# Early start of a second output projection, and other engines for the last products, in a two-layer trunk kernel

## The chip, the cores and the metric

The kernel runs on one core of one Trainium2 chip. Its time is the device time of one execution in microseconds (us), and the number given for it is the median of several runs. A core has a matrix engine (TensorE, PE in the profile; its weight loads are PEld), three engines for the work between the products (VectorE or DVE, ScalarE or ACT, GpSimd or POOL) and SyncE (SP), which here only issues transfers (DMAs). Each engine works through its own queue of instructions in order; semaphores make one engine wait for another. Matmuls write PSUM, eight banks of 128 partitions by 512 floats; the rest of the data lies in SBUF.

## What is computed

A decoder trunk of two residual layers over 1024 tokens with 1024 features, and a final RMS norm. Layer 0 mixes with eight retention heads and eight RWKV-7 heads in parallel; their outputs are concatenated and go through one output projection. Layer 1 uses sliding-window attention. After each mixer comes a SwiGLU FFN.

```python
h = x
for layer in range(DEPTH):
    n = rms_norm(h, norm1_g[layer])
    if layer % 2 == 0:
        mix = retention_rwkv_mixer(n, ...)   # concat([ret_out, rwkv_out]) @ w_out
    else:
        mix = swa_sink_mixer(n, ...)
    h = h + mix
    n = rms_norm(h, norm2_g[layer])
    h = h + swiglu(n, ffn_w_gate[layer], ffn_w_up[layer], ffn_w_down[layer])
return rms_norm(h, final_g)
```

The RWKV group is a recurrence over time, `state = state * w + (state a) b + v k`, with one state of 64 by 64 for each head. The kernel works it out in chunks of 64 tokens. The two parts that the change touches are `concat([ret_out, rwkv_out]) @ w_out` added to `h`, and the final `rms_norm`.

## The kernel before

**Layout.** Everything is held transposed: features on the 128 partitions, tokens along the free axis. The tokens are split into two halves of 512 (`hf` 0 and 1, `HT = 512`), the features into eight blocks of 128 (`KT = 8`). So one block of one half is a tile of 128 by 512 floats, which fills one PSUM bank.

**Products.** Every large product is done in three matmuls on a fast format: an operand is split into a high part (a rounding cast on ScalarE) and a low part (the difference, on GpSimd or VectorE), and `hi*hi + hi*lo + lo*hi` is summed in PSUM. `split` (L339, L341) does this to data and `wsplit` (L318, L319) to weights, 512 columns of a weight at a time into one tile with the tag `w` (four buffers); the raw weights come into `wr` (two buffers of 1024 columns). `gemm` (L333 to L335) does a whole contraction of eight blocks, 24 matmuls; `prod` (L1118 to L1120) does a part of one, told whether it is the first or last part.

**Who orders the work.** The program is written once, in one order, and a planner with a timing model lays out each engine's queue ahead of time. An instruction that comes earlier in the program goes first if its inputs are there, and a later one may fill in. Buffers of a tag (`nq` has four, `f` in PSUM three) are handed out in the order of the program. Pools of tiles open and close like a stack on the left or the right of SBUF; a tile in a new pool waits for the readers of the old tiles that lay in its place.

**Layer 0's mixer** (`mixer0`, L379 to L441). All 16 heads of both halves run under a small schedule of their own (`Plan`). The RWKV heads come in four units `u` of two pairs: (half 0, pairs 0 and 1), (half 0, pairs 2 and 3), then the same for half 1. A unit's recurrence takes eight steps, one after the other; then come a group norm, a gate product and the multiplications at L926 to L928, which leave the output `y` of one pair (two heads) in a tile tagged `rt`. L929 stores it to `cats[hf][4 + p]` in HBM. The retention outputs go to `cats[hf][p]` (L1057). So the eight contraction blocks of half 1's projection are: four of retention, two of unit 2, and two (blocks 6 and 7) of unit 3, the last in time.

**The output projection** (`wout`, L547 to L564) loads the eight head outputs of a half into `nq` tiles, splits them into eight `n8` tiles, loads the residual input (`load8`, L368, on ScalarE's queue) and then does eight output blocks `d`: load and split the weights, `gemm` into a bank of the tag `f`, add to `h` on VectorE (L563).

**What stands around it.** In `trunk` half 0's projection is the last thing in `mixer0`. Then pool `nb` opens, the RMS factor of half 0 is formed (`factor_of`, `rstd`: squares on ScalarE at L349, sums on VectorE at L354, one product with a matrix of ones at L356, then Ln and Exp at L357 and L358; its squares and sums use the same four `nq` buffers), `form0` writes half 0's normalised blocks (L1067), stores them to `bd` (L1078) and splits them, and only then comes `wout(1, ...)`. Behind it are half 1's factor, the first FFN products (`early`, L1266 and L1269) and `form1`, half 1's forms for the FFN (a Strassen-like scheme with seven block products where the plain way has eight).

**The end.** `final_r` (L1541) squares the eight blocks of a half (L1549), scales them by the final gain (L1550), sums seven of the squares on VectorE (L1554), and multiplies the sum (L1557) and the eighth square (L1558) by the ones matrix, then Ln and Exp (L1560, L1561). `final_out` (L1564) multiplies each block by the factor (L1568), on the engine that a letter names (v for VectorE, p for GpSimd), and stores it (L1569). Half 0's factor is formed while the last products of half 1 (`down`) still run; their additions to `h` are at L1305.

```python
K.final_out(0, r0, order[0], "vpvpvpvp")
K.final_out(1, r1, order[1], "vpvvpvvv")
```

Of the kernel before, what the change touches and what calls it, by code (L numbers as in the profile page):

```python
# [13 lines left out]
ALU = mybir.AluOpType  # L14
# [186 lines left out]
class Kern:  # L201
# [172 lines left out]
    @staticmethod  # L374
    def kt(x):
        return lambda k: x[k // 4][:, k % 4, :]


    def mixer0(self):  # L379
# [23 lines left out]
        self.pr, self.st, self.rst, self.dns, self.nds = {}, {}, {}, {}, {}  # L403
# [34 lines left out]
        self.h[0] = self.wout(0, self.n8(self.pp), self.s8(self.hx, "h0", 2))  # L438
        gz.__exit__(None, None, None)
        gm.__exit__(None, None, None)  # L440
        return pq  # L441
# [105 lines left out]
    def wout(self, hf, n8, h8):  # L547

        nc = self.nc
        ch = []  # L550
        for k in range(KT):
            c = self.t(self.pp, [P, HT], "nq", 4)
            nc.sync.dma_start(c, self.cats[hf][k])
            a, b = self.hl(n8, k)
            self.split(c, a, b, k % 2 == 0)
            ch.append((a, b))
        h = self.load8(self.x_half(hf), h8)
        for d in range(KT):
            w = self.wload(self.A["w_out"][d])
            ps = self.pst("f", [P, HT])  # L560
            self.gemm(ps, w, ch)
            hk_ = self.kt(h)(d)
            nc.vector.tensor_tensor(out=hk_, in0=hk_, in1=ps, op=ALU.add)  # L563
        return h  # L564
# [201 lines left out]
    def unit(self, u, hf, pairs):  # L766
# [156 lines left out]
        for p, st, (y, q) in zip(pairs, sts, ys):  # L923
# [5 lines left out]
            nc.sync.dma_start(self.cats[hf][4 + p], y)  # L929
# [611 lines left out]
    def final_r(self, hf, pool, order):  # L1541
# [5 lines left out]
        for i, k in enumerate(order):  # L1547
# [3 lines left out]
            if i == 0:  # L1551
                acc = sq
            elif i < KT - 1:
                nc.vector.tensor_tensor(out=sq, in0=acc, in1=sq, op=ALU.add)  # L1554
                acc = sq
            if i == KT - 2:
                nc.tensor.matmul(ps, self.cst["ones"], acc, start=True, stop=False)  # L1557
        nc.tensor.matmul(ps, self.cst["ones"], sq, start=False, stop=True)  # L1558
# [13 lines left out]
def trunk(tc, A, out):  # L1572
    with ExitStack() as ctx:
        K = Kern(ctx, tc, A, out)

        pq = K.mixer0()
        gb, nb = K.pool("nb", "left")
# [42 lines left out]
        K.form0("n2a", K.factor_of(0, sp, "f"), K.n8(K.pp), sp)  # L1620
        K.h[1] = K.wout(1, K.n8(nb), K.s8(hy, "h1", 2))
# [52 lines left out]
        r0 = K.final_r(0, fz, order[0])  # L1674
        run(f)
        r1 = K.final_r(1, fz, order[1])
        K.final_out(0, r0, order[0], "vpvpvpvp")
        K.final_out(1, r1, order[1], "vpvvpvvv")
# [56 lines left out]
```

## Time and profile before

| | |
|---|---|
| median of 3 runs | 2510.35 us (2509.92 to 2510.72) |
| the profiled execution's own time | 2509.89 us |
| its span in the profile | 2507.3 us |
| granted TensorE clock, mean | 0.974 of full speed |
| VectorE, ScalarE, GpSimd busy | 65%, 41%, 53% of the span |
| the chain that ended last, by engine | PE 65%, DVE 14%, DMA 7%, ACT 5%, issue 4%, POOL 3% |
| DMA | 400.64 MB, mean 160 GB/s |

How to read it. The profile shows one execution. In an order of time, a row gives the start in us from the beginning of the span, the time from the first to the end of the last of the instructions merged in the row, the engine, the line of the kernel, what is written from what, the shape and the count; in square brackets stand the idle time of the engine just before it and what ended it. In the chain that ended last, each row is a piece of time that the end had to wait for: start, length, engine, tile and line. In a table by stretches the columns are the stretch, its length, the busy time and count of each engine, the granted clock, the busy share of the DMA engines and GB/s. Matmuls overlap: one takes 0.39 us from its start to its end, but they follow each other closer than that, so a row's length is not TensorE's pace. `w<-wr` means that a tile tagged `w` was written from one tagged `wr`.

### The profile page before, as it was taken

What the parts mean: (1) busy time and instruction counts of PE and PEld (TensorE: products, weight loads), DVE (VectorE), ACT (ScalarE), POOL (GpSimd) and SP (SyncE); (2) the same over time, 40 slices, a digit from 0 to 9 for tenths busy, and PEclk for the clock granted to TensorE, in tenths of its full rate; (3) what the DMA queues carried; (4) which work ended last, traced back from release to release, by engine and by line L of the source; (5) the groups of instructions that cost most, each with busy time, mean ns of one, the idle gap of its engine ahead of it and who ended that gap; (6) DMA issues with size and microseconds to landing.
All of it is one profiled execution on the core that took longest, in us unless ns stands there. A gap on an engine that the chain in (4) does not pass through costs nothing.

```text
span 2507.3 us, 35752 instructions
## 1 busy us (share of the span) xinstructions
PE 2368.3 (94%) x13106; PEld 1850.0 (74%) x13106; DVE 1631.8 (65%) x2395; ACT 1036.8 (41%) x1907; POOL 1320.2 (53%) x1048
## 2 busy tenths in 40 slices
PE   8899899899978999999999999899998999998996
PEld 6677677677756778887778776677786788886885
DVE  4765854765466248887675358557627788777776
ACT  5354433324354323333333545446634233333335
POOL 6556331312456547776576432252247577767664
PEclk9999999899989999999999999899999999999998
DMA  8565553343353545663464322142335456646652
GB/s 278 186 207 177 178 162 122 117 122 116 116 183 136 192 144 181 219 213 139 174 257 161 97 74 67 42 133 68 109 126 173 146 198 217 219 176 229 243 206 86
DMA packets 169037, 400.64 MB, mean 160 GB/s; under 512 B 43040, under 2 KB 45728, under 8 KB 168864
## 3 DMA queue, kind: packets, MB, share of 16 engines
q1 hardware_dynamic: 165744, 392.87, 45.9%
q10 hardware_dynamic: 2832, 4.45, 0.5%
q8 instruction: 104, 1.70, 0.3%
q0 software_dynamic: 288, 1.05, 0.1%
q14 instruction: 69, 0.57, 0.1%
HBM read 272.34 MB, written 120.59 MB: 157 GB/s over the span
## 4 chain that ended last, share of the span: by engine, by line
PE 65%; DVE 14%; DMA 7%; ACT 5%; issue 4%; POOL 3%; SPq 1%; DVEq 0%; ACTq 0%; POOLq 0%
PE ps_m L1118 5%; PE ps_m L1119 5%; PE ps_m L1120 5%; PE ps_f L232 5%; PE ps_f L334 5%; PE ps_f L333 5%; PE ps_f L335 5%; PE ps_m L232 4%; PE ps_f L1119 3%; PE ps_f L1118 3%; PE ps_f L1120 3%; PE ps_r L1118 2%; PE ps_r L1119 2%; PE ps_r L1120 2%; PE ps_c L1120 2%
## 5 line engine op out<-in xcount | busy, mean ns | idle before, releaser
L319 POOL TENSOR_TENSOR w<-wr,w 128x512 fp32r<-128x512 f32 (+1 forms) x276 | 370.4, 1348 | 475.8 <-ACT w L318 467.2
L232 PE MATMUL ps_f<-n,w 128*128 128x512 f32 x1440 | 388.0, 417 | 5.9 <-ACT n L447 3.7
L232 PEld LDWEIGHTS ps_f<-n,w 128*128 128x128 f32 x1440 | 269.7, 193 | 91.6 <-issue 25.5
L318 ACT CAST w<-wr 128x512 fp32r<-128x512 f32 (+1 forms) x276 | 167.2, 612 | 254.7 <-PE ps_f L335 141.9
L333 PE MATMUL ps_f<-n,w 128*128 128x512 f32 x496 | 200.0, 407 | 10.7 <-ACT n L339 7.7
L334 PE MATMUL ps_f<-n,w 128*128 128x512 f32 x496 | 200.0, 403 | 2.2 <-POOL n L341 1.6
L1118 PE MATMUL ps_f<-n,w 128*128 128x512 f32 x453 | 183.0, 406 | 16.1 <-ACT u L1267 10.6
L335 PE MATMUL ps_f<-n,w 128*128 128x512 f32 x496 | 196.7, 398 | 0.3 <-POOL w L319 0.3
L1119 PE MATMUL ps_f<-n,w 128*128 128x512 f32 x453 | 180.9, 399 | 8.5 <-DVE n L341 5.8
L1120 PE MATMUL ps_f<-n,w 128*128 128x512 f32 x453 | 180.7, 400 | 5.9 <-POOL w L319 5.9
L319 POOL TENSOR_TENSOR w<-wq,w 128x512 fp32r<-128x512 f32 x86 | 124.1, 1453 | 37.5 <-ACT w L318 20.8
L1125 DVE TENSOR_TENSOR nq<-ps_m,u 128x512 f32<-128x512 f32 x88 | 58.7, 684 | 113.3 <-PE ps_m L1120 113.3
L333 PEld LDWEIGHTS ps_f<-n,w 128*128 128x128 f32 x496 | 95.3, 193 | 36.2 <-ACT n L339 9.2
L341 POOL TENSOR_TENSOR n<-nq,n 128x512 fp32r<-128x512 f32 x69 | 115.7, 1688 | 11.0 <-ACT n L339 10.9
L1118 PEld LDWEIGHTS ps_f<-n,w 128*128 128x128 f32 x453 | 86.6, 191 | 46.0 <-ACT u L1267 16.1
L334 PEld LDWEIGHTS ps_f<-n,w 128*128 128x128 f32 x496 | 94.5, 191 | 28.8 <-issue 5.1
L335 PEld LDWEIGHTS ps_f<-n,w 128*128 128x128 f32 x496 | 94.5, 191 | 22.4 <-issue 1.9
L1119 PEld LDWEIGHTS ps_f<-n,w 128*128 128x128 f32 x453 | 86.8, 192 | 29.0 <-DVE n L341 6.5
L1120 PEld LDWEIGHTS ps_f<-n,w 128*128 128x128 f32 x453 | 87.0, 192 | 27.2 <-POOL w L319 7.6
L1118 PE MATMUL ps_m<-cb,w 128*128 128x512 f32 x232 | 93.7, 404 | 9.5 <-DVE nq L1125 9.5
L1279 POOL TENSOR_TENSOR w<-wd,w 128x512 fp32r<-128x512 f32 (+1 forms) x53 | 75.5, 1429 | 49.8 <-ACT w L1278 48.8
L1119 PE MATMUL ps_m<-cb,w 128*128 128x512 f32 x232 | 93.2, 402 | 0.0
(505 smaller groups left out, 6184.4 us busy)
## 6 DMA issues: line engine op xcount, KB each, us to landing
hc<-n SPq DMA_DIRECT2D x74, 512.0 KB, 2.6
wsp<-w SPq DMA_DIRECT2D x60, 512.0 KB, 3.3
w<-wsp SPq DMA_DIRECT2D x60, 512.0 KB, 3.8
wq<-in_w_gate SPq DMA_DIRECT2D x44, 512.0 KB, 4.4
u<-u SPq DMA_DIRECT2D x88, 256.0 KB, 2.9
n<-hc SPq DMA_DIRECT2D x43, 512.0 KB, 5.8
hid<-n SPq DMA_DIRECT2D x66, 256.0 KB, 2.1
ha<-hc SPq DMA_DIRECT2D x33, 512.0 KB, 6.0
```

The lines of the kernel that those rows point to most:

```text
L232: self.nc.tensor.matmul(out, lhsT, rhs, **kw)
L318: nc.scalar.copy(hi[:, :n], raw[:, c])
L319: nc.gpsimd.tensor_tensor(out=lo[:, :n], in0=raw[:, c], in1=hi.bitcast(F32)[:, :n], op=ALU.subtract)
L333: nc.tensor.matmul(ps, hi, rh, start=k == 0, stop=False)
L334: nc.tensor.matmul(ps, hi, rl, start=False, stop=False)
L335: nc.tensor.matmul(ps, lo, rh, start=False, stop=k == n - 1)
L341: e.tensor_tensor(out=lo, in0=src, in1=hi.bitcast(F32), op=ALU.subtract)
L1118: mm(ps, hi, xh, start=first and k == 0, stop=False, skip_group_check=True)
L1119: mm(ps, hi, xl, start=False, stop=False, skip_group_check=True)
L1120: mm(ps, lo, xh, start=False, stop=last and k == len(w) - 1, skip_group_check=True)
L1125: add = lambda o, x, y: V.tensor_tensor(out=o, in0=x, in1=y, op=ALU.add)
L1279: nc.gpsimd.tensor_tensor(out=lo, in0=v, in1=hi.bitcast(F32), op=ALU.subtract)
```

## The change

It has three parts.

1. **Head outputs.** The loading and splitting of the heads leaves `wout` and becomes `heads(hf, n8, have)`. For half 1 it is called at the end of `mixer0`, right after half 0's projection and before the pool of the mixer closes, so in the program it now stands before half 0's RMS factor. The two outputs of unit 3 are not stored to HBM and loaded again: their `rt` tiles are kept in `self.last` and split in place.
2. **Half 1's projection.** `wout(1, ch, ..., 2)` begins with three output blocks over the first six contraction blocks: `d = 0` and `1` over blocks 0 to 3, both over 4 and 5, then `d = 2` over 0 to 5; then all three over blocks 6 and 7; then the additions. The weights of `d = 0` and `1` are loaded and split in halves of 512 columns, so that both first halves come first. The other five blocks are done as before. The ones product of half 0's factor takes the PSUM tag `m` (four banks) in place of `f`, whose three banks the three open outputs hold.
3. **The end.** For half 1 only four squares are summed on VectorE; the other four go to the ones matrix one by one. All of half 0's last products go to GpSimd, and of half 1's one more.

```diff
@@ mixer0
-        self.h[0] = self.wout(0, self.n8(self.pp), self.s8(self.hx, "h0", 2))
+        self.h[0] = self.wout(0, self.heads(0, self.n8(self.pp)), self.s8(self.hx, "h0", 2))
         gz.__exit__(None, None, None)
+        gb, nb = self.pool("nb", "left")
+        ch = self.heads(1, self.n8(nb), self.last)
         gm.__exit__(None, None, None)
-        return pq
+        return pq, gb, nb, ch
@@ heads, wout
-    def wout(self, hf, n8, h8):
-
-        nc = self.nc
+    def heads(self, hf, n8, have=None):
+
         ch = []
         for k in range(KT):
-            c = self.t(self.pp, [P, HT], "nq", 4)
-            nc.sync.dma_start(c, self.cats[hf][k])
+            c = (have or {}).get(k)
+            if c is None:
+                c = self.t(self.pp, [P, HT], "nq", 4)
+                self.nc.sync.dma_start(c, self.cats[hf][k])
             a, b = self.hl(n8, k)
             self.split(c, a, b, k % 2 == 0)
             ch.append((a, b))
+        return ch
+
+    def wout(self, hf, ch, h8, late=0):
+
+
+        nc = self.nc
         h = self.load8(self.x_half(hf), h8)
-        for d in range(KT):
+        kt = self.kt(h)
+
+        def add(d, ps):
+            nc.vector.tensor_tensor(out=kt(d), in0=kt(d), in1=ps, op=ALU.add)
+
+        n = 3 if late else 0
+        if late:
+            parts = []
+            for o in (0, HT):
+                raw = self.t(self.pp, [P, 1024], "wr", 2)
+                for d in range(2):
+                    nc.sync.dma_start(raw[:, d * HT : d * HT + HT], self.A["w_out"][d][:, o : o + HT])
+                parts.append([self.wsplit(raw[:, d * HT : d * HT + HT], HT) for d in range(2)])
+            w = [parts[0][d] + parts[1][d] for d in range(2)] + [self.wload(self.A["w_out"][2])]
+            ps = [self.pst("f", [P, HT]) for _ in range(3)]
+            k = KT - late
+            for d, ks in ((0, (0, 4)), (1, (0, 4)), (0, (4, k)), (1, (4, k)), (2, (0, k)), *((d, (k, KT)) for d in range(3))):
+                c = slice(*ks)
+                self.prod(ps[d], w[d][c], ch[c], ks[0] == 0, ks[1] == KT)
+            for d in range(3):
+                add(d, ps[d])
+        for d in range(n, KT):
             w = self.wload(self.A["w_out"][d])
             ps = self.pst("f", [P, HT])
             self.gemm(ps, w, ch)
-            hk_ = self.kt(h)(d)
-            nc.vector.tensor_tensor(out=hk_, in0=hk_, in1=ps, op=ALU.add)
+            add(d, ps)
         return h
@@ unit
-            nc.sync.dma_start(self.cats[hf][4 + p], y)
+            if u < 3:
+                nc.sync.dma_start(self.cats[hf][4 + p], y)
+            else:
+                self.last[4 + p] = y
@@ final_r(self, hf, pool, order, n)
-            if i == 0:
-                acc = sq
-            elif i < KT - 1:
+            if 0 < i < n:
                 nc.vector.tensor_tensor(out=sq, in0=acc, in1=sq, op=ALU.add)
-                acc = sq
-            if i == KT - 2:
-                nc.tensor.matmul(ps, self.cst["ones"], acc, start=True, stop=False)
-        nc.tensor.matmul(ps, self.cst["ones"], sq, start=False, stop=True)
+            acc = sq
+            if i >= n - 1:
+                nc.tensor.matmul(ps, self.cst["ones"], sq, start=i == n - 1, stop=i == KT - 1)
@@ trunk
-        pq = K.mixer0()
-        gb, nb = K.pool("nb", "left")
+        pq, gb, nb, ch = K.mixer0()
...
-        K.form0("n2a", K.factor_of(0, sp, "f"), K.n8(K.pp), sp)
-        K.h[1] = K.wout(1, K.n8(nb), K.s8(hy, "h1", 2))
+        K.form0("n2a", K.factor_of(0, sp, "m"), K.n8(K.pp), sp)
+        K.h[1] = K.wout(1, ch, K.s8(hy, "h1", 2), 2)
...
-        r0 = K.final_r(0, fz, order[0])
+        r0 = K.final_r(0, fz, order[0], 7)
         run(f)
-        r1 = K.final_r(1, fz, order[1])
-        K.final_out(0, r0, order[0], "vpvpvpvp")
-        K.final_out(1, r1, order[1], "vpvvpvvv")
+        r1 = K.final_r(1, fz, order[1], 4)
+        K.final_out(0, r0, order[0], "pppppppp")
+        K.final_out(1, r1, order[1], "vpvvpvvp")
```

More of the change, by code (lines that the diff above doesn't have):

```diff
@@ L402, in mixer0 @@
         pq = self.psum("ps0", {"f": 3, "m": 4, "c": 1})
-        self.pr, self.st, self.rst, self.dns, self.nds = {}, {}, {}, {}, {}
+        self.pr, self.st, self.rst, self.dns, self.nds, self.last = {}, {}, {}, {}, {}, {}
         units = [(0, 0), (0, 2), (1, 0), (1, 2)]
@@ L1539, in w_o, with final_r @@
             )
-    def final_r(self, hf, pool, order):
+    def final_r(self, hf, pool, order, n):
         nc = self.nc
```

## The prediction

> **What bounds the kernel now.** I read the page first, then the chain that ended last between 590 and 860 us and from 2400 us on, then each engine's order of time at those two places.
>
> ```profile
> span 2507.3 us, 35752 instructions
> PE 2368.3 (94%) x13106; PEld 1850.0 (74%) x13106; DVE 1631.8 (65%) x2395; ACT 1036.8 (41%) x1907; POOL 1320.2 (53%) x1048
> ```
>
> TensorE (PE) is busy for 94%, so at most 139 us can be had by closing its gaps. The change touches two: the start of the second output projection and the end of the kernel. The first, in TensorE's order of time:
>
> ```profile
> 705.67 0.39 PE L335 MATMUL ps_f<-n,w 128*128 128x512 f32 x1
> 710.47 2.07 PE L356 MATMUL ps_f<-nq,c_ones 128*128 128x512 f32 x2 [4.41 <-DVE nq L354]
> 720.22 1.22 PE L333 MATMUL ps_f<-n,w 128*128 128x512 f32 x2 [7.67 <-ACT n L339]
> ```
>
> ```profile
> 769.42 0.39 PE L1118 MATMUL ps_f<-n,w 128*128 128x512 f32 x1
> ```
>
> The first projection issues its last matmul at 705.67 and ends at 705.9. The second begins at 720.2, when ScalarE (ACT) has cast its first head output, and gives way to the FFN at 769.4. Why so late, in SyncE's queue (SPq), ScalarE's order and the chain:
>
> ```profile
> 661.38 0.33 SPq L1057 DMA_DIRECT2D cat<-r  x1
> 667.59 32.90 SPq L293 DMA_DIRECT2D wr<-in_w_out  x6
> 703.58 5.21 SPq L929 DMA_DIRECT2D cat<-rt  x2
> 708.91 0.86 SPq L1205 DMA_DIRECT2D wq<-in_w_gate  x2
> 709.82 1.69 SPq L553 DMA_DIRECT2D nq<-cat  x3
> ```
>
> ```profile
> 668.76 1.15 ACT L349 ACTIVATE nq<-h 128x512 f32<-128x512 f32 x2
> ...
> 719.55 2.37 ACT L339 CAST n<-nq 128x512 fp32r<-128x512 f32 x4
> ```
>
> ```profile
> 707.75 0.69 DVE rt L928
> 708.43 0.61 DVE h L563
> 709.06 0.64 ACT nq L349
> 709.73 0.70 DVE nq L354
> ```
>
> The last retention output was stored at 661.4, yet even it is read back only after 709.8: the loads share the four `nq` buffers with the RMS sum of half 0, which comes first in the program and ends at 710.4 (L354). The last RWKV output is ready at 708.4 (L928). So two of eight contraction blocks are late, and six wait for buffers. The same time by stretches (length, then busy PE, PEld, DVE, ACT, POOL, granted clock, DMA share, GB/s):
>
> ```profile
> 660.00:706.00 46.00, 46.00 (x288) 34.83 (x283) 18.70 (x34) 21.15 (x31) 16.96 (x14) 1.00 0.37 126
> 710.00:720.00 10.00, 2.07 (x2) 0.50 (x2) 5.17 (x6) 6.42 (x9) 3.28 (x2) 0.50 1.04 396
> 720.00:726.00 6.00, 5.36 (x12) 3.77 (x13) 6.00 (x7) 2.44 (x6) 3.38 (x3) 0.50 0.86 287
> ```
>
> After the gap TensorE works 6 us at half clock, so the gap costs more than its length.
>
> **The change at the projection.** An output block takes 24 matmuls; two successive additions show its length when nothing is in the way:
>
> ```profile
> 758.74 0.69 DVE L563 TENSOR_TENSOR h<-h,ps_f 128x512 f32<-128x512 f32 x1 [2.83 <-PE ps_f L335]
> 764.18 0.69 DVE L563 TENSOR_TENSOR h<-h,ps_f 128x512 f32<-128x512 f32 x1 [2.83 <-PE ps_f L335]
> ```
>
> That is 5.44 us, 0.2267 a matmul, 43.5 for all 192. The new order does 54 of them first (three outputs over six blocks, 12.2 us), then 18 over the last two (4.1), then five outputs as before (27.2). If TensorE never waits, it runs on from 705.9: plus 43.5, plus the RMS matmul pair (2.07 at half clock above, so 1.0 at full) gives 750.4 instead of 769.4, a gain of 19.0.
>
> What must hold:
>
> *The six early heads.* Loads, casts and subtractions move ahead of the RMS sum. With a store and a load of about this landing time,
>
> ```profile
> hid<-n SPq DMA_DIRECT2D x66, 256.0 KB, 2.1
> ```
>
> the last one is back by 666, and the squares of half 0 begin at 668.8 now: the sum is hardly held up, and it has until 706 to catch up. The work is 6 casts of 0.6 on ScalarE, 3 subtractions on GpSimd (POOL) and 3 on VectorE (DVE) of at most 1.7 (rows below). It lies beside the first projection, 660 to 706, where TensorE is busy 46.00 of 46.00 and the three engines under half. Without that cover it costs at most 5 us. In SyncE's queue the loads pass the six projection weight loads and two of the FFN's; 1.5 MB at a DMA share of 0.37 is hidden. Two stores and two loads go.
>
> *The two late heads.* Split in place behind L928: a cast of 0.6 and a subtraction of at most 1.7 put the last at 710.7, and the late block is not reached before 718. That covers 7 us.
>
> *Weights.* Two of four weight loads become pairs of 256 KB, and two split tiles stay held until the late block. One half of the fourth output's weights waits for such a tile, released near 720; its cast and subtraction may stand behind one of half 0's forms:
>
> ```profile
> L319 POOL TENSOR_TENSOR w<-wr,w 128x512 fp32r<-128x512 f32 x18 | 25.1, 1404 | 22.4 <-ACT w L318 22.4
> L341 POOL TENSOR_TENSOR n<-u,n 128x512 fp32r<-128x512 f32 x4 | 6.9, 1730 | 10.5 <-ACT n L339 10.5
> ```
>
> 720 + 0.6 + 1.7 + 1.4 is 723.7, for a tile wanted at 722.6 or 725.3. Bounds 0 to 5 us; I take 3 with all small waits, as these rows miss by one at least.
>
> *Half 1's input* must have landed for the first addition, near 720:
>
> ```profile
> L368 ACTq DMA_DIRECT2D h<-in_xT x2: 374/374/374, 706.2 to 709.1; - x2
> ```
>
> ```profile
> DMA to landing us min/median/max: 5.0/7.2/9.3
> ```
>
> 718.4 at the latest now; 2 MB of head loads no longer crowd it, and its space is read 2 us longer. Nothing added. The RMS pair's new PSUM tag has buffers free since L928, before the pair can run: nothing.
>
> Gain: 19.0 - 3 = **16.0 us**. The work behind starts from the second projection's last addition, so I carry the gain to the end undiminished.
>
> On a wait that stays, the Trainium skill ("TensorE: Matmul & The Clock Gate", What's actually happening) says that about 3.4 us of sustained work restore the full clock. The rows here show some 6. A new idle stretch would so cost 1.7 us extra by the page (an estimate) and 3.0 by the rows; the rows decide.
>
> **The change at the end.** VectorE (two stretches), TensorE, ScalarE (two) and GpSimd (two) now:
>
> ```profile
> 2479.87 5.76 DVE L1568 TENSOR_TENSOR h<-h,y 128x512 f32<-128x512 f32 x4 [3.41 <-ACT y L1561]
> ```
>
> ```profile
> 2491.54 0.68 DVE L1305 TENSOR_TENSOR h<-h,ps_y 128x512 f32<-128x512 f32 x1
> 2497.81 5.84 DVE L1568 TENSOR_TENSOR h<-h,y 128x512 f32<-128x512 f32 x6 [5.59 <-ACT y L1561]
> ```
>
> ```profile
> 2483.44 0.39 PE L1120 MATMUL ps_y<-n,w 128*128 128x512 f32 x1
> ```
>
> ```profile
> 2492.25 0.63 ACT L1549 ACTIVATE nq<-h 128x512 f32<-128x512 f32 x1 [0.60 <-DVE h L1305]
> ```
>
> ```profile
> 2497.15 0.63 ACT L1561 ACTIVATE y<-y 128x512 f32<-128x512 f32 x1
> ```
>
> ```profile
> 2449.05 1.29 POOL L341 TENSOR_TENSOR n<-hr,n 128x512 fp32r<-128x512 f32 x1
> ```
>
> ```profile
> 2479.92 6.83 POOL L1568 TENSOR_TENSOR h<-h,y 128x512 f32<-128x512 f32 x4 [6.59 <-ACT y L1561]
> ```
>
> TensorE is done at 2483.8, but the last addition to half 1 runs at 2491.5, since four products of half 0 stand before it on VectorE. They go to GpSimd: the addition can run from 2483.8 to 2484.5. ScalarE has earlier squares and scalings to finish (0.5 late), then needs the same 5.5 us from the last square's start to the factor's end (2492.25 to 2497.78): 2485.0 + 5.5 is 2490.5 instead of 2497.8. The last four squares go to TensorE one by one, pairs of at most 2.1 us, as they arrive; the last pair lies in those 5.5 us as now.
>
> Then the last products, five on VectorE, three on GpSimd. GpSimd has eight of half 0 first, from 2479.9: 10.3 us at 1.29 alone, 13.7 at 1.71 (6.83/4) beside VectorE's. VectorE does additions from PSUM meanwhile, not those products, so I take 10.3: free at 2490.2. Three more at 1.71 end at 2495.6; VectorE's five at 1.44 (5.76/4) beside them and 0.7 after take some 6 us, to 2496.5. Now the last ends at 2503.65. Gain **7.2 us**; by the other bound 2498.9 and 4.8.
>
> The Trainium skill ("GPSIMD Engine Reference", Engine selection) speaks against this edit: for elementwise work it advises VectorE, GpSimd being about 2 times slower with two inputs. The rows agree, 1.29 against 0.68. By the page's factor eleven products of 1.36 (an estimate) would end at 2494.9, still before VectorE.
>
> **Sum.** 16.0 + 7.2 = 23.2 off the profiled execution's own 2509.89 (its span and 2.6 around it). That lies 0.46 under the median of 2510.35, hence **2487.2**.
>
> **The rivals.**
>
> *The banks.* Three outputs hold all three `f` PSUM banks; the fourth needs the first one's addition, on a VectorE queue that also carries half 0's forms, held up by a store. In the chain and in VectorE's order:
>
> ```profile
> 719.02 4.90 DMA bd<-u
> ```
>
> ```profile
> 728.26 3.47 DVE L341 TENSOR_TENSOR n<-u,n 128x512 fp32r<-128x512 f32 x2
> ```
>
> Behind them, at 731.7, output four starts at 732.4, not 723: 9.3 lost and 3.0 of half clock, 2499.5. For: VectorE is busy 6.00 of 6.00 from 720 to 726. Against: four of the head subtractions leave that stretch.
>
> *The change doesn't do what it says:* if the new tiles become free only with the last head's, at 708.4, six casts and three subtractions hold TensorE until about 712, some 6 and 1 of half clock: 2494.2. Against: their space is what the retention part and the inner pool leave, done by 661.4.
>
> *The FFN swallows it.* Half 1's forms keep VectorE full after the projection:
>
> ```profile
> 800.00:810.00 10.00, 6.48 (x15) 4.57 (x15) 10.00 (x9) 4.31 (x8) 8.72 (x6) 0.58 0.31 109
> ```
>
> TensorE waits here and falls to 0.58. If this stretch ended when it does now, only 7.2 would stay: 2503.2, give or take 3. Against: it starts from half 1's factor, which waits for the projection.
>
> *GpSimd ends last*, at 2498.9: 2489.6.
>
> *Slower.* TensorE takes its queue in order, so the first of the 18 late matmuls blocks all behind it. If the last head's split stood behind half 0's forms, the price is 1 us for each beyond 718 and 3 of half clock. It eats the 23 when the split lands at 738 and ends slower by over 0.2% beyond 743: 2516 or more. For: it needs the same two queues; the forms' end at 731.7, a second wait of 4.9 for a store and its own 2.3 are 739. Against: it is ready at 708.4, before any form.
>
> **How the numbers follow.** Forecast 0.53, GpSimd last 0.07, banks 0.16, not done as said 0.07, FFN 0.12, slower 0.05. A measurement here tells some 0.2%, 5 us, from no change: the bound for faster is 2505.3. FFN lies half on each side of it: faster 0.89, same 0.06, slower 0.05. The forecast's own bounds, 0 to 5 for the small waits and 1 at the tail, give 2484 to 2490. The range goes to 2482, since waits behind the projection may fall by 2, and up to 2500 to hold the banks; the FFN and the slower case, 0.17, are left out.
>
> **What would show it.** No TensorE gap over 2 us between 706 and 751, clock 1.00; first L1118 at 751 to 755; the six head loads before 670; the last addition within 1 us of TensorE's last product, the last multiplication about 13 us after it instead of 20. Wrong would be: TensorE waiting in the late block for the split, a fourth output waiting for a bank, or the shift at L1118 not found again at the end.

## The result and the profile after

The changed kernel takes 2485.91 us (median of 4 runs, 2481.93 to 2489.24) beside 2510.53 (4 runs, 2509.92 to 2511.55): a ratio of 0.9901, 95% interval 0.9884 to 0.9918, or 24.6 us less. The forecast was 2487.2 us.

The page of the profiled execution (2481.93 us):

```profile
span 2480.2 us, 35757 instructions
PE 2357.5 (95%) x13112; PEld 1844.5 (74%) x13112; DVE 1623.6 (65%) x2387; ACT 1036.0 (42%) x1907; POOL 1324.5 (53%) x1053
```

TensorE is busy for 10.8 us less than before (2368.3) and idle for 16.3 us less; the span is 27.1 us shorter. The line numbers have moved: L341, L349 and L356 are as before, the additions of the projection are now L570 (L563 before), half 0's forms L1099 (L1067), the products of `prod` L1150 to L1152 (L1118 to L1120), the last multiplications L1598 (L1568).

TensorE at the join of the two projections, in order of time: the last four products of the RWKV heads' gates, the first product of the second projection, half 0's RMS pair, the one gap, the FFN's first product:

```profile
695.05 1.88 PE L232 MATMUL ps_m<-gl,gup 128*128 128x512 f32 x4
...
700.41 0.39 PE L1150 MATMUL ps_f<-n,w 128*128 128x512 f32 x1
...
707.62 1.13 PE L356 MATMUL ps_m<-nq,c_ones 128*128 128x512 f32 x2
...
721.43 0.47 PE L333 MATMUL ps_f<-n,w 128*128 128x512 f32 x1 [3.39 <-ACT n L339]
...
748.76 0.39 PE L1150 MATMUL ps_f<-n,w 128*128 128x512 f32 x1
```

The second projection starts in the matmul after the first one's last, not 14 us later, and passes half 0's RMS pair, which runs at 707.62 behind its first 31 products. The gap of 3.39 us comes at the fourth output, behind the late block. The row names a cast as what ended it, but VectorE shows what the output had to wait for, a free `f` bank:

```profile
711.84 3.78 DVE L1099 SCALAR_TENSOR_TENSOR u<-h,pv,rs 128x512 f32<-128x512 f32 x4 [4.28 <-ACT rs L358]
715.55 3.47 DVE L341 TENSOR_TENSOR n<-u,n 128x512 fp32r<-128x512 f32 x2
718.94 1.74 DVE L1099 SCALAR_TENSOR_TENSOR u<-h,pv,rs 128x512 f32<-128x512 f32 x1
720.61 0.67 DVE L570 TENSOR_TENSOR h<-h,ps_f 128x512 f32<-128x512 f32 x1
```

The first addition to half 1, which empties the first of the three banks, stands behind seven of half 0's forms and subtractions. It ends at 721.28; TensorE goes on at 721.43.

What feeds the early start, in the changed kernel: SyncE's last three loads of early heads, and then, on ScalarE, the last early head's cast and the last late one's:

```profile
658.22 3.88 SPq L556 DMA_DIRECT2D nq<-cat  x3
```

```profile
668.75 0.60 ACT L339 CAST n<-nq 128x512 fp32r<-128x512 f32 x1
...
704.23 0.62 ACT L339 CAST n<-rt 128x512 fp32r<-128x512 f32 x1 [2.28 <-DVE rt L957]
```

The last of the six early heads is cast at 668.75, 31 us before it is wanted; the last head in place at 704.23, against its use in the late block near 714 (54 products of 0.2267 and the RMS pair after 700.41).

The end of the kernel: TensorE's last product, VectorE, ScalarE's last square, GpSimd.

```profile
2461.98 0.39 PE L1152 MATMUL ps_y<-n,w 128*128 128x512 f32 x1
```

```profile
2462.40 0.69 DVE L1337 TENSOR_TENSOR h<-h,ps_y 128x512 f32<-128x512 f32 x1 [0.32 <-PE ps_y L1152]
2470.11 6.30 DVE L1598 TENSOR_TENSOR h<-h,y 128x512 f32<-128x512 f32 x5 [7.02 <-ACT y L1591]
```

```profile
2463.49 0.61 ACT L1582 ACTIVATE nq<-h 128x512 f32<-128x512 f32 x1
2464.14 0.72 ACT L1583 ACTIVATE h<-h,pv 128x512 f32<-128x512 f32 x1
2464.76 0.61 ACT L1582 ACTIVATE nq<-h 128x512 f32<-128x512 f32 x1
2465.41 0.72 ACT L1583 ACTIVATE h<-h,pv 128x512 f32<-128x512 f32 x1
2466.15 1.28 ACT L1590 ACT_TABLE_LOAD   x1
```

```profile
2458.45 10.38 POOL L1598 TENSOR_TENSOR h<-h,y 128x512 f32<-128x512 f32 x8 [6.59 <-ACT y L1591]
2470.15 5.11 POOL L1598 TENSOR_TENSOR h<-h,y 128x512 f32<-128x512 f32 x3 [1.32 <-ACT y L1591]
```

The last addition follows the last product at once, and the last multiplication ends 14.0 us after that addition began (2476.41 less 2462.40). ScalarE now works without a pause; its last square starts 1.7 us after the addition has ended.

**Where the time went.** For every kernel I read the same marks from its trace. *Lead-in*: from the span's start to the first product of the first output projection, which no kernel here changes. *Projection*: from the start of the last gate product (0.59 us before the end of the row at 695.05) to ScalarE's first copy of an FFN product (`u<-ps_f`, at 751.68 in the trace after); it holds the join, the second projection and the FFN's first product, 55.34 us here. *Tail*: from the start of TensorE's last product to the span's end. In us, with the medians of all runs and the ratio to the kernel before on the same chip:

| kernel | lead-in | projection | tail | span | median (runs) | ratio, 95% interval |
|---|---|---|---|---|---|---|
| before | 627.8 | 70.97 | 23.89 | 2507.3 | 2510.53 (4) | |
| after | 624.0 | 55.34 | 18.18 | 2480.2 | 2485.91 (4) | 0.9901, 0.9884-0.9918 |
| after again | 630.9 | 56.86 | 18.19 | 2493.6 | 2487.24 (4) | 0.9920, 0.9895-0.9944 |
| tail only | 627.2 | 71.01 | 18.49 | 2497.6 | 2501.71 (7) | 0.9971, 0.9958-0.9984 |
| projection only | 625.8 | 55.30 | 24.84 | 2491.3 | 2497.67 (6) | 0.9962, 0.9946-0.9978 |
| in place, plain order | 622.4 | 58.42 | 18.63 | 2488.5 | 2490.43 (4) | 0.9933, 0.9918-0.9948 |
| through HBM, late block | 623.0 | 58.21 | 19.14 | 2486.9 | 2489.89 (4) | 0.9928, 0.9900-0.9955 |
| through HBM, plain order | 621.0 | 55.00 | 18.55 | 2477.1 | 2484.47 (4) | 0.9919, 0.9888-0.9950 |
| two in place, six late | 626.8 | 72.99 | 18.73 | 2501.6 | 2503.39 (10) | 0.9969, 0.9950-0.9987 |
| sum in other buffers | 624.1 | 70.00 | 18.47 | 2491.9 | 2504.63 (10) | 0.9976, 0.9960-0.9992 |
| sum in an `f` bank | 626.3 | 61.82 | 18.18 | 2490.8 | 2494.61 (4) | 0.9952, 0.9933-0.9970 |
| two open outputs | 622.8 | 53.42 | 18.47 | 2478.8 | 2487.52 (4) | 0.9919, 0.9889-0.9949 |
| ... and scaling on VectorE | 625.1 | 53.44 | 21.14 | 2490.6 | 2490.99 (5) | 0.9924, 0.9896-0.9951 |
| ... and scaling behind squares | 625.8 | 53.41 | 21.07 | 2491.6 | 2489.29 (4) | 0.9909, 0.9877-0.9942 |

The projection is 15.6 us shorter (14.1 in the second profile of the same kernel), the tail 5.7. That is 21.3 (19.8) of the 27.1 us. 3.8 of the rest was already there at the end of the lead-in, and the two profiles of one and the same kernel differ by 6.9 us there. So an experiment here is judged by its stretch, which the two profiles of one kernel give within 1.5 us, before its median. From the copy that ends the stretch to VectorE's first addition in `late` (`nq<-ps_m,u`) it is 143.64 us before and 143.30 after, so nothing is lost there. From the same copy to TensorE's last product it is 1711.1 before and 1710.3 after, but 1715.3 in the second profile. The ten kernels with a projection under 62 us take 1713.6 there in the mean, the four others 1709.5. So whether some 4 us of the gain are given back behind the projection is not settled: these traces hint at it, while by their medians the same ten gain as much, in the mean, as projection and tail together.

### The profile page after: what moved, and what is told of

The parts are those of the page before. It is cut to its first block, busy times and chain, and to the rows that moved or that the text cites. A ratio compares the mean times of both kernels' runs of the same rounds, so it can differ in the third digit from the quotient of the medians.

```text
span 2480.2 us, 35757 instructions
## 1 busy us (share of the span) xinstructions
PE 2357.5 (95%) x13112; PEld 1844.5 (74%) x13112; DVE 1623.6 (65%) x2387; ACT 1036.0 (42%) x1907; POOL 1324.5 (53%) x1053
## 4 chain that ended last, share of the span: by engine, by line
PE 66%; DVE 14%; DMA 6%; ACT 5%; issue 4%; POOL 3%; SPq 1%; DVEq 0%; ACTq 0%; POOLq 0%
PE ps_m L1150 5%; PE ps_m L1152 5%; PE ps_m L1151 5%; PE ps_f L232 5%; PE ps_f L334 4%; PE ps_f L333 4%; PE ps_f L335 4%; PE ps_m L232 4%; PE ps_f L1151 3%; PE ps_f L1150 3%; PE ps_f L1152 3%; PE ps_r L1151 2%; PE ps_r L1150 2%; PE ps_r L1152 2%; PE ps_c L1152 2%
## 5 line engine op out<-in xcount | busy, mean ns | idle before, releaser
L1150 PE MATMUL ps_f<-n,w 128*128 128x512 f32 x477 | 192.4, 405 | 15.9 <-ACT u L1299 10.6
L1152 PE MATMUL ps_f<-n,w 128*128 128x512 f32 x477 | 190.4, 401 | 5.9 <-POOL w L319 5.9
L333 PE MATMUL ps_f<-n,w 128*128 128x512 f32 x472 | 188.1, 400 | 6.4 <-ACT n L339 3.4
L334 PE MATMUL ps_f<-n,w 128*128 128x512 f32 x472 | 188.4, 399 | 0.3 <-POOL n L341 0.3
L335 PE MATMUL ps_f<-n,w 128*128 128x512 f32 x472 | 186.5, 396 | 0.3 <-POOL w L319 0.3
L1150 PEld LDWEIGHTS ps_f<-n,w 128*128 128x128 f32 x477 | 91.2, 191 | 46.5 <-ACT u L1299 16.0
L341 POOL TENSOR_TENSOR n<-nq,n 128x512 fp32r<-128x512 f32 x68 | 111.7, 1653 | 12.2 <-ACT n L339 12.2
L1152 PEld LDWEIGHTS ps_f<-n,w 128*128 128x128 f32 x477 | 91.5, 192 | 28.3 <-POOL w L319 7.6
L333 PEld LDWEIGHTS ps_f<-n,w 128*128 128x128 f32 x472 | 89.3, 190 | 29.0 <-ACT n L339 3.8
L334 PEld LDWEIGHTS ps_f<-n,w 128*128 128x128 f32 x472 | 89.0, 188 | 24.0 <-issue 4.8
L335 PEld LDWEIGHTS ps_f<-n,w 128*128 128x128 f32 x472 | 89.0, 189 | 21.5 <-issue 2.1
L1150 PE MATMUL ps_m<-cb,w 128*128 128x512 f32 x232 | 93.3, 402 | 9.5 <-DVE nq L1157 9.5
```

Of the source, the lines that this page charges most:

```text
L333: nc.tensor.matmul(ps, hi, rh, start=k == 0, stop=False)
L334: nc.tensor.matmul(ps, hi, rl, start=False, stop=False)
L335: nc.tensor.matmul(ps, lo, rh, start=False, stop=k == n - 1)
L341: e.tensor_tensor(out=lo, in0=src, in1=hi.bitcast(F32), op=ALU.subtract)
L1150: mm(ps, hi, xh, start=first and k == 0, stop=False, skip_group_check=True)
L1152: mm(ps, lo, xh, start=False, stop=last and k == len(w) - 1, skip_group_check=True)
```

## The experiments

### The parts by themselves

*After again* is the changed kernel once more.

> The changed kernel as it is, once more, for a second trace and for the spread of its time. The first trace lies 3.8 us ahead of the one of before already at 620 us, where both kernels still have the same order of instructions. Theory (chance of the execution): this lead is another one here, between 4 us ahead and 4 us behind, and the time falls in 2482 to 2489. Rival (the change moves something there too): the same 3.8 us again. In both, second projection to FFN about 16 us earlier against the point at 627, and a wait of 2 to 4 us between the late block and the fourth output.

*Tail only* is the kernel before with the diff's `final_r` and `final_out` parts:

```diff
+        r0 = K.final_r(0, fz, order[0], 7)
...
+        r1 = K.final_r(1, fz, order[1], 4)
+        K.final_out(0, r0, order[0], "pppppppp")
+        K.final_out(1, r1, order[1], "vpvvpvvp")
```

> Only the end is changed (fewer sums on VectorE, half 0's last products all on GpSimd); the projection is as before. Theory (the two gains add): 5.8 us faster than before, 2504.7, all of it behind TensorE's last product. Rival (the tail's gain comes only because the projection's shift changes what meets there): under 2 us.

*Projection only* is all the rest of the diff.

> Heads early, two split in place, three outputs opened over six blocks; the end is as before. Theory: 16 us faster than before plus or minus the chance of the first 620 us (4): 2494, and the first FFN product 16 us earlier than before, counted from the first projection's start. Rival (the FFN swallows it): the shift is there at the first FFN product and less than 8 us of it is left at the kernel's last matmul.

The tail alone is worth 5.7 us by the medians (2501.71 against 2507.45 in that series) and 5.4 by its stretch. The projection alone has the same stretch as with the tail, 55.30, with the same gap:

```profile
723.24 0.47 PE L333 MATMUL ps_f<-n,w 128*128 128x512 f32 x1 [3.37 <-ACT n L339]
```

Its median gains only 9.8 us, less than the 12 at least that was expected. The repeat of the changed kernel has its median in the expected 2482 to 2489, but its runs reach from 2480.86 to 2495.35. What was expected of the times was too narrow for this kernel's spread. By the stretches the two parts add up: 15.7 and 5.4 alone, 15.6 and 5.7 together. By the medians they are 9.8 and 5.7 alone and 20.2 together in the same series; the intervals are wide enough for both readings.

### Split in place, and the order of the late block

The change brings two ways to cover the late heads: no round trip through HBM, and three outputs begun with six blocks. Four kernels make a square of them; the six early heads and the tail are in all. *In place, plain order*:

```diff
-        K.h[1] = K.wout(1, ch, K.s8(hy, "h1", 2), 2)
+        K.h[1] = K.wout(1, ch, K.s8(hy, "h1", 2))
```

> As the changed kernel, but the second projection goes one output after the other over all eight blocks, as before; heads early and two split in place. Theory (the loads ahead of the RMS sum and the split in place make the gain, the new order adds nothing): TensorE reaches block 7 of the first output 4.8 us after the first projection, and the split is done 5.2 us after it, so it waits under 1 us; the wait of 3.4 us for a PSUM bank goes, too. Same time as the changed kernel or 2 to 3 us less. Rival (the order is what fills the gap): TensorE waits 5 us or more in the first output and falls to half clock, 6 to 8 us more than the changed kernel.

*Through HBM, late block* stores the last two outputs and loads them back into `rt` tiles:

```diff
...
-            if u < 3:
-                nc.sync.dma_start(self.cats[hf][4 + p], y)
-            else:
-                self.last[4 + p] = y
+            nc.sync.dma_start(self.cats[hf][4 + p], y)
```

> The changed kernel, but the last two head outputs of half 1 are stored and loaded back as before the change; the order of three opened outputs stays. Segment from the last product of the first mixer's gates to the first copy of the first FFN product (70.97 us before, 55.34 after, 58.42 with the plain order and the split in place). Theory (the order alone covers the round trip): the halves come ready some 6 us later, near 710 to 711 on the changed kernel's own clock, and the late block is reached near 712, so the segment is 55 to 57 us and the time within 2 us of the changed kernel. Rival (the split in place is needed): the late block waits for the loads or, behind them in SyncE's order, for the loads of half 1's x and of the weights, with a PE gap of 3 us or more and the granted clock down after it: 60 to 66 us, 5 to 11 us slower.

*Through HBM, plain order* has both edits, so that the early heads and the pair's bank `m` are all that is left of the projection's part.

> The last two head outputs stored and loaded back, and the second projection in its plain order; only the six early heads and the second bank pool are left of the projection's part. Theory (each of the two parts covers the wait by itself): the first output reaches its seventh block some 3.5 us after its start, well before the halves, and TensorE waits 5 us or more there and falls to half clock for some 6 us: segment 63 to 68 us, 5 to 9 us over the plain order with the split in place (58.42). Rival (neither part matters, the early six heads do it all): 57 to 60 us, as the plain order with the split in place.

| projection stretch, us | late block | plain order |
|---|---|---|
| in place | 55.34, 56.86 | 58.42 |
| through HBM | 58.21 | 55.00 |

Taking one of the two away costs 1.4 to 3.1 us in these profiles, taking both away costs nothing. With one profile of each of the three, and 1.5 us between the two of the changed kernel, the small differences are not sure, and the medians don't separate the four. Neither the theory nor the rival met the first two kernels, which came out between them. For the last kernel both fell, 63 to 68 and 57 to 60. Its heads do come back late, cast on ScalarE at 701.25 and 706.19:

```profile
701.25 0.63 ACT L339 CAST n<-rt 128x512 fp32r<-128x512 f32 x1 [1.93 <-DMA rt<-cat]
...
706.19 0.62 ACT L339 CAST n<-rt 128x512 fp32r<-128x512 f32 x1 [2.85 <-DMA rt<-cat]
```

But TensorE doesn't stand still there, in its own order of time in this kernel:

```profile
706.12 0.40 PE L335 MATMUL ps_f<-n,w 128*128 128x512 f32 x1
706.36 0.40 PE L334 MATMUL ps_f<-n,w 128*128 128x512 f32 x1
706.86 0.49 PE L333 MATMUL ps_f<-n,w 128*128 128x512 f32 x1
```

One output's products go L333, L334, L335 and again. Here a L335 is followed by L334, and L333 comes after that: two outputs lie interleaved. The count says the same. When the last head is cast at 706.19, TensorE has begun 34 products of the second projection, and the first output has only 21 without its last block. The planner, which may fill in a later instruction when an earlier one's input is late, has by itself opened the second output while the first waits for its last block. It does unasked what the late block writes out.

What each of the four then pays is a wait of another kind. In place with the plain order there are two for weights, since ScalarE's casts for the fourth output's weights stand behind half 0's:

```profile
718.38 0.50 PE L333 MATMUL ps_f<-n,w 128*128 128x512 f32 x1 [1.78 <-ACT w L318]
721.68 0.80 PE L335 MATMUL ps_f<-n,w 128*128 128x512 f32 x1 [2.58 <-POOL w L319]
```

Through HBM with the late block it is the bank wait of the changed kernel, longer:

```profile
721.85 0.47 PE L333 MATMUL ps_f<-n,w 128*128 128x512 f32 x1 [4.91 <-DVE h L573]
```

```profile
721.03 1.27 DVE L573 TENSOR_TENSOR h<-h,ps_f 128x512 f32<-128x512 f32 x2
```

With both edits it is a bank again, after an addition that ends at 718.25:

```profile
718.40 0.47 PE L333 MATMUL ps_f<-n,w 128*128 128x512 f32 x1 [2.78 <-ACT n L339]
```

```profile
717.58 1.27 DVE L573 TENSOR_TENSOR h<-h,ps_f 128x512 f32<-128x512 f32 x2
```

So near 718 to 722 each version stops at the fourth output: three are done, and what the next stands on (a bank, or weights) comes when VectorE and ScalarE get past half 0's forms.

### What the gain hangs on

*Two in place, six late* leaves the two late heads in place, but calls the loads of the six others where they were, behind half 0's RMS sum and forms; the call in `mixer0` is left with blocks 6 and 7:

```diff
...
-        K.h[1] = K.wout(1, ch, K.s8(hy, "h1", 2), 2)
+        K.h[1] = K.wout(1, K.heads(1, n8h, None, range(6)) + ch, K.s8(hy, "h1", 2))
```

> The changed kernel with the last two head outputs split in place, but the other six loaded and split where they were before the change in the program, behind half 0's RMS sum, and the second projection written in its plain order. Theory (the six early heads make the whole gain of the projection): their four buffers come free only when the sum is done, so TensorE has a gap of 10 us or more ahead of the second projection, and the segment from the gates' last product to the FFN's first copy is 66 to 72 us (70.97 before, 55 to 58 in the variants with early heads). Rival (the split in place has a share of its own): 60 to 65 us. The tail stays at 18.2 to 18.7.

```profile
705.35 4.17 SPq L557 DMA_DIRECT2D nq<-cat  x3
...
720.59 2.56 SPq L557 DMA_DIRECT2D nq<-cat  x2
```

```profile
709.23 2.07 PE L356 MATMUL ps_m<-nq,c_ones 128*128 128x512 f32 x2 [5.79 <-DVE nq L354]
718.97 1.22 PE L333 MATMUL ps_f<-n,w 128*128 128x512 f32 x2 [7.67 <-ACT n L339]
```

The loads wait for the sum's tiles again, TensorE has its two gaps of before, and the stretch is 72.99: the whole gain is gone, 14.6 us against the kernel that differs in the six heads alone (58.42). It was expected to be 72 at most.

*Sum in other buffers* is *tail only* with one thing new: half 0's sum takes four `u0` tiles, not the `nq` tiles that the head loads use.

```diff
...
-        K.form0("n2a", K.factor_of(0, sp, "f"), K.n8(K.pp), sp)
+        K.form0("n2a", K.factor_of(0, sp, "f", (sp, [P, HT], "u0", 4)), K.n8(K.pp), sp)
```

> The kernel before the change with the changed tail; its projection as it was, all eight heads stored and loaded, loads behind half 0's RMS sum in the program. Only this is new: the sum takes its tiles from another tag than the head loads (four tiles that half 0's forms use later). Theory (what held the six loads back was the shared buffers, not their place in the program, since the planner lets a later instruction fill in when its inputs and its buffer are there): SyncE issues six loads before 670 and the segment is 55 to 60 us. Rival (the place in the program counts, or the new tiles come free late and hold up the sum): 64 us or more, with the loads or the squares of half 0 behind 700.

SyncE now issues the six loads early without their being moved in the program, and ScalarE has cast them by 668.3. But the squares of half 0 start only at 703.89, and TensorE waits for the sum with six heads ready. That the new tiles lie in space which is read until then would explain the late start; the trace names no wait that shows it. The last four squares stand on ScalarE behind the cast of the last head, which waits for its load until 712.64:

```profile
658.27 3.88 SPq L553 DMA_DIRECT2D nq<-cat  x3
```

```profile
667.05 1.25 ACT L339 CAST n<-nq 128x512 fp32r<-128x512 f32 x2
...
703.89 2.38 ACT L349 ACTIVATE u<-h 128x512 f32<-128x512 f32 x4
712.64 0.62 ACT L339 CAST n<-nq 128x512 fp32r<-128x512 f32 x1 [6.37 <-DMA nq<-cat]
```

```profile
717.02 2.08 PE L356 MATMUL ps_f<-u,c_ones 128*128 128x512 f32 x2 [16.37 <-DVE u L354]
```

The stretch, 70.00, is the rival's, but both theories hold half: the shared buffers, not the place in the program, had held back the loads; and early heads alone are worth 1 us here, since the RMS pair (`ps_f`) stands ahead of all the projection in TensorE's queue. That points at a word of the change that had been counted at nothing, the sum's bank. *Sum in an `f` bank* undoes it in the changed kernel:

```diff
-        K.form0("n2a", K.factor_of(0, sp, "m"), K.n8(K.pp), sp)
+        K.form0("n2a", K.factor_of(0, sp, "f"), K.n8(K.pp), sp)
```

> The changed kernel with one word undone: half 0's RMS sum takes its PSUM bank from tag f again, as before the change, not from m. The prediction counted this part at nothing. Theory (it is a necessary part: the f banks are handed out in program order, so with the sum's pair in f the second projection's products stand behind the pair in TensorE's queue, as they did in the run with the sum in other buffers): TensorE stops for 6 to 7 us at the end of the first projection, until the sum is ready, with the clock down after it; some of this is paid back by the bank gap of 3.4 us, so the segment is 59 to 64 us against 55.3 and 56.9. Rival (the part is worth nothing): 54 to 57 us, no gap ahead of the second projection. If the theory holds, the prediction's term of nothing for this tag was wrong, though its sum came out.

```profile
709.84 2.08 PE L356 MATMUL ps_f<-nq,c_ones 128*128 128x512 f32 x2 [7.00 <-DVE nq L354]
```

```profile
706.00:712.00 6.00, 2.16 (x3) 1.13 (x4) 2.40 (x4) 3.10 (x5) 2.03 (x2) 0.50 0.94 321
```

TensorE stops for 7.00 us at the end of the first projection and runs at half clock after it. The stretch is 61.82, and no other gap follows: the word is worth 5.0 to 6.5 us against the two profiles of the changed kernel. The `f` banks are handed out in the order of the program; with the pair in `m` the projection, later in the program, may pass it. Whether the sum's tiles and its bank together would do without moving the heads was not tried.

### The bank wait

*Two open outputs* lets the late block begin two outputs, not three; its lists and loops over three go over `n`:

```diff
-        n = 3 if late else 0
+        n = 2 if late else 0
...
```

> The changed kernel with two outputs opened by the late block instead of three; the third keeps the plain order, so one of the three banks is free when the late block ends. Theory (the 3.39 us gap at 721 is a wait for a bank, which the first addition frees, held up by half 1's x and by VectorE's queue): the gap goes or shrinks below 1 us, the segment is 52 to 53 us, 2 to 3 us faster than the changed kernel. Rival (the next output is late in any case, by its weights, or the gap moves to the output after it): the segment stays at 54 to 57 us; and if the late block, now begun some 4 us earlier, comes ahead of the split, a gap appears there.

```profile
727.10 0.50 PE L335 MATMUL ps_f<-n,w 128*128 128x512 f32 x1 [1.02 <-POOL w L319]
```

```profile
714.52 1.27 DVE L570 TENSOR_TENSOR h<-h,ps_f 128x512 f32<-128x512 f32 x2
```

Two outputs are done earlier, the planner puts their additions ahead of half 0's subtractions at 714.52, and the bank gap is gone; 1.02 us for weights remain. The stretch is 53.42, a little over the 52 to 53 of the theory, and 53.44 and 53.41 in the two kernels below that share this edit: 1.9 to 3.4 us less than the changed kernel, the smallest of all. In the medians (2487.52 against 2485.91 and 2487.24) it can't be told apart from it, as 2 us are less than their spread.

### The tail

*... and scaling on VectorE* also moves half 1's last four multiplications by the final gain off ScalarE:

```diff
+            if i < n:
+                nc.scalar.activation(h(k), h(k), AF.Copy, scale=self.col("nf", k))
+            else:
+                nc.vector.tensor_scalar(out=h(k), in0=h(k), scalar1=self.col("nf", k), scalar2=None, op0=ALU.mult)
```

> The kernel with two opened outputs, and half 1's last four multiplications by the final gain on VectorE instead of ScalarE. Theory (the 1.3 us that the tail lost to its forecast lie in ScalarE's own order of square, scaling, square): from the last product to the end 18.2 us becomes 16.5 to 17.2. Rival (VectorE's additions of the last outputs come later, behind its multiplications, or GpSimd's products of 1.29 us set the end): 18 us or more.

```profile
2465.47 10.93 POOL L1601 TENSOR_TENSOR h<-h,y 128x512 f32<-128x512 f32 x8 [6.59 <-ACT y L1594]
```

```profile
2471.30 1.35 DVE L1586 TENSOR_SCALAR h<-h,pv 128x512 f32<-128x512 f32 x1 [0.70 <-ACT nq L1582]
2472.56 0.67 DVE L1337 TENSOR_TENSOR h<-h,ps_f 128x512 f32<-128x512 f32 x1
2473.93 1.34 DVE L1586 TENSOR_SCALAR h<-h,pv 128x512 f32<-128x512 f32 x1 [0.70 <-ACT nq L1582]
...
2476.63 0.48 DVE L1586 TENSOR_SCALAR h<-h,pv 128x512 f32<-128x512 f32 x1 [0.76 <-ACT nq L1582]
```

The rival holds, and worse: a chain has come about, addition, square on ScalarE, scaling on VectorE, next addition, some 2.6 us an output where ScalarE took 1.3 (2463.49 to 2464.76). The tail is 21.14. *... and scaling behind squares* writes the last three scalings behind the last square:

```diff
...
+        for k in order[n + 1 :]:
+            nc.vector.tensor_scalar(out=h(k), in0=h(k), scalar1=self.col("nf", k), scalar2=None, op0=ALU.mult)
```

> The kernel with two opened outputs, and the last three multiplications by the final gain taken off ScalarE and done by VectorE behind the last addition, in the time in which it waits for the factor (the earlier trial on VectorE had them between the additions, 21.14 us from the last product to the end). Theory (ScalarE's series of squares, scalings and table loads sets the factor's end: each scaling taken from it is worth 0.72 us): the factor ends some 2 us earlier, the three multiplications of 1.35 us beside GpSimd fit before it, and the tail is 16.0 to 16.8 us instead of 18.2 to 18.5. Rival (VectorE is not free by then, or the planner puts them between the additions again): 18 us or more.

The planner puts them between the additions all the same, as each has its input by then, and the tail is 21.07:

```profile
2471.41 1.34 DVE L1591 TENSOR_SCALAR h<-h,pv 128x512 f32<-128x512 f32 x1 [1.38 <-ACT nq L1582]
```

That ScalarE's series sets the factor's end is not shown by these two, since VectorE's chain took its place; it is argued from the trace after, where ScalarE has no pause from 2463.49 until its table load at 2466.15.

## Why the prediction was right, and where it was not

The sum, 23.2 us, was 21.3 and 19.8 by the two places in two profiles, 24.6 and 20.2 by the medians. Of the prediction's own signs, the second projection followed at once, the late block did not wait for the split, and the last addition and multiplication came as said. But the sign of no gap over 2 us failed, and one that it named as a sign of being wrong came true: the fourth output waited for a bank. Step by step:

- **The gap that closes**, at most 19.0, less 3: 15.6 and 14.1 in the two profiles, right. TensorE's last matmul of the first projection is followed at once by the second, and in the first profile the shift lasts to the end of TensorE's work (1711.1 us before, 1710.3 after). The FFN did not swallow the gain; a loss of some 4 us behind the projection is not excluded.
- **The six early heads**: loads and casts were hidden as worked out, and the gain needs them: without them 14.6 us are lost.
- **The RMS pair's new PSUM tag, "nothing"**: this is the step that failed. It cost nothing, but the 19.0 rested on it: in `f` the pair holds back the whole projection for 7.00 us, 5.0 to 6.5 in the stretch. The prediction asked whether a bank would be free, not what would have to stand behind the pair.
- **The two late heads**: the split in place came in time, as predicted, but no gain of its own is shown. The prediction took the written order for TensorE's order; the planner opens a second output unasked, and the stretch is 55.00 without the split in place and without the late block.
- **Small waits, 3 us**: the size was right (3.39), the place wrong. It was charged to weights for the fourth output; there it was the bank, the rival priced at 9.3 and 3.0 of half clock. The rival's mechanism came true at about a third of its price: the addition came at 720.61, not behind all forms at 731.7 (the first projection's last matmul starts 5.5 us earlier here, at 700.18, so on the prediction's clock it is 726.1); the clock stayed up in one profile and fell in the other. The weight waits do show in other versions (1.78 and 2.58; 1.02).
- **The tail, 7.2**: 5.7, 1.5 too much. GpSimd's eight products took 10.38 us as taken (10.3), its three 5.11 (5.1) and VectorE's five 6.30 (some 6). Mis-sized was ScalarE: its last square starts 2.4 us after TensorE's end (2464.76 less 2462.37), not 1.2, as each output costs it a square and a scaling, 1.27 us, and the additions come faster.
- **GpSimd ends last**: no. Its three products end 1.15 us before VectorE's five. (From the prediction's own figures, eleven products of 1.71 after 2479.9, that bound is 2498.7, not 2498.9.)

The forecast fell within 1.3 us of the median partly by luck: a tail term 1.5 too large, a wait of the right size from another cause, and runs of one kernel that lie 14.5 us apart.

## What to carry to other kernels

Before an order is written out by hand, see whether the planner already makes it: here two shared resources held it back, each shown by itself, the four `nq` tiles and the `f` banks. An instruction that shares a buffer tag with later work is a gate for that work even if a buffer is free, so a step that "moves a small matmul to another bank" has to be costed by what stands behind it. Where runs differ by more than the effect, compare the stretch between two fixed marks in the traces, and look at an unchanged stretch first.

## What the runs showed of the hardware

**Short gaps and the clock.** The table by stretches has the granted clock as the third number from the end. Here it is for the 4 us behind the gap near 720, for the changed kernel (a gap of 3.39 us), for the same kernel again (3.35, seven us later), for through HBM with the late block (4.91), and for in place with the plain order (1.78 and 2.58, with 0.7 us of matmuls between):

```profile
722.00:726.00 4.00, 4.00 (x19) 3.30 (x18) 4.00 (x4) 3.07 (x6) 4.00 (x3) 1.00 0.79 277
```

```profile
728.00:732.00 4.00, 3.70 (x10) 2.96 (x11) 4.00 (x5) 3.33 (x7) 3.71 (x3) 0.57 0.73 241
```

```profile
722.00:726.00 4.00, 4.00 (x11) 3.14 (x12) 3.90 (x5) 3.06 (x6) 3.29 (x4) 0.57 0.73 252
```

```profile
722.00:726.00 4.00, 4.00 (x12) 3.12 (x12) 4.00 (x4) 0.62 (x1) 4.00 (x3) 0.64 0.32 104
```

The same gap in the same program left the clock at 1.00 in one execution and took it to 0.57 in the other. In 4 us at 0.57 some 1.7 us of work are lost (4 times 0.43), which is about the 1.5 us between the two profiles' stretches. The Trainium skill ("TensorE: Matmul & The Clock Gate", What's actually happening) says that the clock goes down after an idle window of about 3.4 us, and that the window runs freely. That agrees with a gap of this length going either way. A single gap of 2.78 us (through HBM, plain order) left it at 1.00. The two short gaps, in one trace, show that a few matmuls in between need not keep the clock up.

**A scaling beside GpSimd.** VectorE's TENSOR_SCALAR took 1.35 and 1.34 us while GpSimd multiplied, from 2465.47 to 2476.40, and 0.48 when it had finished (the rows at 2465.47, 2471.30, 2473.93 and 2476.63 above). The additions from PSUM between them took 0.67 throughout. The Trainium skill ("SBUF — State Buffer", SBUF: two separate sides) says that VectorE and GpSimd share a pair of ports that one instruction holds for its whole length, and names for VectorE two-input operations and those in a two-port mode; the rows agree in kind, and show that this one-input scaling is slowed too.

**One program, two lead-ins.** The changed kernel reached its first projection after 624.0 us in one profile and 630.9 in another. What makes the difference is open.
